# Dilated attention with tokens in class order from psum on; gamma products on VectorE

## The chip, the cores and the metric

The kernel runs on one core of one Trainium2 chip. The time is the device time of that core in microseconds (us); lower is better. Engines are named as in the profile: PE (TensorE), DVE (VectorE), ACT (ScalarE), POOL (GpSimd), SP (SyncE, which issues most transfers).

## What is computed

One sequence of 512 tokens with 1024 features passes through two blocks in fp32. The first block has a layer with an RWKV-7 and a MoBA mixer, a squared-ReLU MLP, a layer of dilated attention and another MLP. The second block has four mixers side by side (S5, HGRN2, FoX, mLSTM), an output projection and a SwiGLU layer. Two places matter here.

Dilated attention has 8 heads of 128 features, and for each head three queries, one for each pair of span and dilation, (128, 1), (512, 4) and (2048, 16), with one key and one value:

```python
q, k = _partial_rotary(q, pos), _partial_rotary(kv[0], pos)
for g, (span, dilation) in enumerate(DIL_PAIRS):
    o, l = _dilated_window_branch(q[:, g], k, v, span, dilation)
wts = jax.nn.softmax(jnp.stack(lses, axis=0), axis=0)
o = jnp.einsum('gbht,gbhtd->bhtd', wts, jnp.stack(outs, axis=0))
```

With dilation 4 a token sees tokens of its own class, its position mod 4; with dilation 16, of its own class mod 16. The rotary part turns the first 32 of the 128 features.

In the second block each branch ends in a norm with gain: `h = h + rms_norm(mix, ln_mix_post)` after the output projection, and `h = h + rms_norm(ff, ln_ffn_post)` at the end, where `rms_norm` is x times the reciprocal root of the mean square, times gamma.

## The kernel before

All large projections are done as three fp32r matmuls for each 128 x 512 product (high part by high, high by low, low by high; lines 272 to 274, 249 to 251, 356 to 358). Weights come by DMA on SP's queue into `wr`, ACT rounds them to the high part `wh` (L228), and DVE or POOL subtracts for the low part `wl` (L230).

In `dilated` (L1215) the projections of the eight heads are a stream of tasks on PE, five for a head, in the order key, three queries, value (j = 3, 0, 1, 2, 4). Each task's result in psum is copied out by ACT into `dz` (`evac`, L1228). For queries and the key the rotary part follows on the first 32 partitions: DVE shuffles halves into `dsh` (L1238), POOL multiplies `dsh` by the sines (L1243), DVE multiplies `dz` by the cosines (L1244), POOL adds the two (L1245). Before, only the query of dilation 1 (j = 0) is stored by class: within each tile of 128 tokens first the 32 tokens of class 0, then of class 1 and so on, so its copy (L1233) and its products have operands with steps of four fp32. The others lie in the order of the tokens.

`head` (L1250) then does one head. It transposes the value (`dipv`, L1257). For each tile t of 128 queries `score` makes a row of scores in psum, `disc`: one matmul with the near keys (L1265), and for the two dilated queries four small matmuls each, one for a class r, which write 32 psum partitions and 32 (t + 1) columns (L1268). Both operands of these are read with a step of four fp32:

```python
lhsT=q[:, t * P + r : t * P + P : 4], rhs=k[:, r : 4 * n : 4], start=True, stop=True,
tile_position=(0, 32 * r),
```

DVE adds the mask and takes the maximum (L1284), ACT does the exponential (L1290), and DVE makes the weights `e` over all keys of the tiles up to t (`de`): reciprocal (L1292), class masks scaled (L1294), the sum of the two dilated parts (L1295), its spread to four classes (L1297), and the near part (L1301). PE transposes `e` (`dipt`, L1305), DVE and ACT copy the halves (`dpt`, L1310 and L1311), and PE multiplies with the value (`dipo`, L1314). ACT writes the head's output back in token order with a step of four (L1316). The order on PE is set by a small planner (`race`, L305) that puts the steps of a head between matmuls of the projection stream; the numbers that a head yields are its estimates. Each engine executes in a fixed order of its own.

`post_part` (L1005) handles one half (c = 0 or 1, 512 features) of one tile of 128 tokens of a branch: ACT squares it and sums the squares (`square`, L990); for c = 0 ACT copies it from psum (L1012, if the destination is another tile) and POOL multiplies by gamma in place (L1013), for c = 1 DVE multiplies (L1017). `post_norm` (L1020) takes the reciprocal root on DVE (`rsqrt1`, lines 166 to 174) and adds both halves into the residual stream (L1029). It serves the output projection of the second block, whose four tiles of the half c = 0 are finished in psum early (`K.po`), and the SwiGLU layer, whose sums `facc` lie in SBUF. The transposes for the next projection are `ptr` (L980).

Of the kernel before, what the change touches and what calls it, by code (L numbers as in the profile page):

```python
# [15 lines left out]
ALU = mybir.AluOpType  # L16
# [27 lines left out]
def make_consts():  # L44
# [28 lines left out]
    q_ = (4 * ii + cc)[:, None]  # L73
    neg = lambda ok: np.where(ok, 0.0, NEG)
    add("dil", "cls", cc[:, None] == np.arange(4))
    for t in range(NT):
        n = 32 * (t + 1)
        j = np.arange(n)[None, :]
        i_ = (32 * t + ii)[:, None]
        own = neg(c_ <= q_)  # L80
        near = own if t == 0 else np.concatenate([neg(c_ >= q_), own], 1)
        add("dil", f"dil{t}", np.concatenate([near, neg(j <= i_), neg((j <= i_) & ((i_ - j) % 4 == 0))], 1))
# [828 lines left out]
class Stream:  # L911
# [93 lines left out]
    def post_part(self, pool, t, c, src, g, dst):  # L1005
# [4 lines left out]
        if c == 0:  # L1010
            if dst is not src:
                self.K.nc.scalar.copy(dst, src)  # L1012
            self.K.nc.gpsimd.tensor_tensor(dst, dst, g[:, 0:512], op=ALU.mult)  # L1013
        else:
            if dst is src:
                dst = pool.tile([P, 512], F32, name="sg")
            self.K.nc.vector.tensor_tensor(dst, src, g[:, 512:D], op=ALU.mult)  # L1017
# [197 lines left out]
def dilated(K, ctx, S, x, win, rope_d, yT, ys, w_out):  # L1215
# [12 lines left out]
    def evac(h, j):  # L1228
        def f(ps):
            z = s2.tile([P, T], F32, name=f"dz{j}")  # L1230
            if j == 0:
                z4 = z.rearrange("p (t r i) -> p t r i", t=NT, r=4)
                nc.scalar.copy(z4, ps.rearrange("p (t i r) -> p t r i", t=NT, r=4))  # L1233
            else:
                nc.scalar.copy(z, ps)
            if j < 4:
                sh = s2.tile([32, T], F32, name="dsh")
                nc.vector.stream_shuffle(sh, z[0:32], swap)  # L1238
                zr, sr, c_, s_ = z[0:32], sh, rope[:, 0, :], rope[:, 1, :]
                if j == 0:  # L1240
                    zr, sr = z4[0:32], sh.rearrange("p (t r i) -> p t r i", t=NT, r=4)
                    c_, s_ = (a.rearrange("p (t i r) -> p t r i", t=NT, r=4) for a in (c_, s_))
                nc.gpsimd.tensor_tensor(sr, sr, s_, op=ALU.mult)  # L1243
                nc.vector.tensor_tensor(zr, zr, c_, op=ALU.mult)  # L1244
# [5 lines left out]
    def head(h, L):  # L1250
        while any((h, j) not in R for j in range(5)):
            yield None
        k, q0, q1, q2, vt = (R[h, j] for j in (3, 0, 1, 2, 4))
        v = s2.tile([P, NT, P], F32, name="dv")
# [6 lines left out]
        def score(t):  # L1261
# [4 lines left out]
            for g, q in ((0, q1), (1, q2)):  # L1266
                for r in range(4):
                    nc.tensor.matmul(  # L1268
                        ps[32 * r : 32 * r + 32, n0 + g * n : n0 + g * n + n],
                        lhsT=q[:, t * P + r : t * P + P : 4], rhs=k[:, r : 4 * n : 4], start=True, stop=True,  # L1270
# [1113 lines left out]
```

## Time and profile before

| | |
|---|---|
| median of the runs | 2234.99 us (3 runs, 2234.35 to 2239.33) |
| the profiled execution, its own time | 2230.15 us |
| its span, first to last instruction | 2228.0 us |
| PE busy | 2160.5 us (97%) |
| DVE busy | 1265.1 us (57%) |
| ACT busy | 758.6 us (34%) |
| POOL busy | 382.0 us (17%) |
| mean granted clock of PE | 0.987 of 2.4 GHz |
| chain that ended last | PE 79%, DVE 10%, issue 4%, ACT 3%, DMA 2%, POOL 2% |

Busy time is the time in which an engine executes instructions of the program. The chain that ended last is followed back from the last instruction, at each step to what released it. A row of a timeline has the start in us from the span's start, the length in us, the engine, the line, the operation, the tiles out<-in, shapes and the number of records; in brackets, how long the engine had been idle and what released it. A PE row of x16 is sixteen records in a row, and an fp32 matmul has two records. The granted clock is what the chip allows PE: 1.00 is 2.4 GHz, 0.50 is 1.2 GHz. A row of busy time by stretch has the stretch's start and end and its length, then the busy us (and records) of PE, of PEld (PE's weight loads), DVE, ACT and POOL, then the mean granted clock, the busy share of the DMA engines and the GB/s that they moved. A row of the groups by line has, behind the shapes and the count, the busy us and the mean ns of one, and then the us of idle time before them; in the groups of a stage, the waits are a total, their number and the longest, in us.

### The profile page before, as it was taken

What the parts mean: (1) busy time and instruction counts of PE and PEld (TensorE: products, weight loads), DVE (VectorE), ACT (ScalarE), POOL (GpSimd) and SP (SyncE); (2) the same over time, 40 slices, a digit from 0 to 9 for tenths busy, and PEclk for the clock granted to TensorE, in tenths of its full rate; (3) what the DMA queues carried; (4) which work ended last, traced back from release to release, by engine and by line L of the source; (5) the groups of instructions that cost most, each with busy time, mean ns of one, the idle gap of its engine ahead of it and who ended that gap; (6) DMA issues with size and microseconds to landing.
All of it is one profiled execution on the core that took longest, in us unless ns stands there. A gap on an engine that the chain in (4) does not pass through costs nothing.

```text
span 2228.0 us, 37413 instructions
## 1 busy us (share of the span) xinstructions
PE 2160.5 (97%) x15646; PEld 1709.3 (77%) x15646; DVE 1265.1 (57%) x2528; ACT 758.6 (34%) x1218; POOL 382.0 (17%) x399
## 2 busy tenths in 40 slices
PE   8999999999999999999999999998999998999997
PEld 6666667888878877777788888877667778888886
DVE  6576666764444765656574444466755566344445
ACT  4332333423322433333342233235434354222221
POOL 0011111370056242332130000011320021000001
PEclk9999999999999999999999999998899999999999
DMA  4111114342333322222243233213211232233321
GB/s 142 49 40 40 49 40 170 97 131 95 100 100 113 126 77 67 67 68 66 86 139 94 90 104 95 93 45 132 63 45 46 92 104 95 95 97 98 99 76 38
DMA packets 56088, 192.80 MB, mean 87 GB/s; under 512 B 8208, under 2 KB 8720, under 8 KB 55408
## 3 DMA queue, kind: packets, MB, share of 16 engines
q1 hardware_dynamic: 52384, 184.11, 25.6%
q0 software_dynamic: 3536, 6.32, 0.9%
q8 instruction: 122, 2.00, 0.4%
q14 instruction: 46, 0.38, 0.1%
HBM read 181.98 MB, written 8.39 MB: 85 GB/s over the span
## 4 chain that ended last, share of the span: by engine, by line
PE 79%; DVE 10%; issue 4%; ACT 3%; DMA 2%; POOL 2%; SPq 0%; DVEq 0%; ACTq 0%; POOLq 0%
PE gemm L272 6%; PE mlpo L356 6%; PE mlpo L357 6%; PE mlpo L358 6%; PE gemm L273 5%; PE gemm L274 5%; PE mlps L249 4%; PE mlps L250 4%; PE mlps L251 4%; PE ffg L250 2%; PE ffg L251 2%; PE ffg L249 2%; PE ffu L250 2%; PE ffu L251 2%; PE ffu L249 2%
## 5 line engine op out<-in xcount | busy, mean ns | idle before, releaser
L228 ACT CAST wh<-wr 128x1024 fp32r<-128x1024 f32 (+1 forms) x311 | 323.4, 1044 | 762.3 <-PE mlpo L358 247.5
L230 DVE TENSOR_TENSOR wl<-wr,wh 128x1024 fp32r<-128x1024 f32 (+1 forms) x285 | 354.9, 1246 | 359.9 <-ACT wh L228 270.2
L272 PE MATMUL gemm<-acth,wh 128*128 128x512 f32 (+1 forms) x672 | 306.1, 456 | 7.8 <-ACT acth L238 6.4
L274 PE MATMUL gemm<-acth,wl 128*128 128x512 f32 (+1 forms) x672 | 271.8, 404 | 4.5 <-DVE wl L230 4.5
L273 PE MATMUL gemm<-actl,wh 128*128 128x512 f32 (+1 forms) x672 | 272.4, 405 | 0.0
L356 PE MATMUL mlpo<-wh,mlph 128*128 128x512 f32 x688 | 270.2, 393 | 0.3 <-DVE xres L1039 0.3
L357 PE MATMUL mlpo<-wl,mlph 128*128 128x512 f32 x688 | 269.6, 392 | 0.0
L358 PE MATMUL mlpo<-wh,mlpl 128*128 128x512 f32 x688 | 269.4, 392 | 0.0
L249 PE MATMUL mlps<-acth,wh 128*128 128x512 f32 x448 | 176.3, 394 | 0.0
L251 PE MATMUL mlps<-acth,wl 128*128 128x512 f32 x448 | 176.2, 393 | 0.0
L250 PE MATMUL mlps<-actl,wh 128*128 128x512 f32 x448 | 176.1, 393 | 0.0
L272 PEld LDWEIGHTS gemm<-acth,wh 128*128 128x128 f32 (+1 forms) x672 | 128.9, 192 | 59.1 <-issue 24.7
L274 PEld LDWEIGHTS gemm<-acth,wl 128*128 128x128 f32 (+1 forms) x672 | 128.9, 192 | 36.0 <-DVE wl L230 5.8
L356 PEld LDWEIGHTS mlpo<-wh,mlph 128*128 128x128 f32 x688 | 129.4, 188 | 29.3 <-DVE xres L1039 0.4
L358 PEld LDWEIGHTS mlpo<-wh,mlpl 128*128 128x128 f32 x688 | 129.1, 188 | 29.1 <-DVE mlpl L239 0.2
L357 PEld LDWEIGHTS mlpo<-wl,mlph 128*128 128x128 f32 x688 | 129.2, 188 | 28.6
L230 POOL TENSOR_TENSOR wl<-wr,wh 128x1024 fp32r<-128x1024 f32 (+1 forms) x26 | 71.2, 2763 | 446.0 <-ACT wh L228 424.1
L273 PEld LDWEIGHTS gemm<-actl,wh 128*128 128x128 f32 (+1 forms) x672 | 129.9, 193 | 22.9 <-issue 4.4
L1039 DVE SCALAR_TENSOR_TENSOR xres<-xres,mlpo 128x512 f32<-128x512 f32 x120 | 82.1, 685 | 105.3 <-PE mlpo L358 104.3
L251 PEld LDWEIGHTS mlps<-acth,wl 128*128 128x128 f32 x448 | 84.1, 188 | 19.7
L250 PEld LDWEIGHTS mlps<-actl,wh 128*128 128x128 f32 x448 | 84.2, 188 | 19.4
L249 PEld LDWEIGHTS mlps<-acth,wh 128*128 128x128 f32 x448 | 84.1, 188 | 19.5
(617 smaller groups left out, 3901.9 us busy)
## 6 DMA issues: line engine op xcount, KB each, us to landing
wr<-mlp_w SPq DMA_DIRECT2D x128, 512.0 KB, 3.6
wr<-ffn_w SPq DMA_DIRECT2D x66, 512.0 KB, 3.5
wr<-c_w_in SPq DMA_DIRECT2D x40, 512.0 KB, 3.6
wr<-ab_w_in SPq DMA_DIRECT2D x25, 512.0 KB, 3.6
wr<-w_in SPq DMA_DIRECT2D x24, 512.0 KB, 3.7
wr<-ab_w_out SPq DMA_DIRECT2D x8, 512.0 KB, 3.9
wr<-c_w_out SPq DMA_DIRECT2D x8, 512.0 KB, 3.7
wr<-w_out SPq DMA_DIRECT2D x8, 512.0 KB, 3.9
```

The costliest lines, as they stand in the source:

```text
L228: nc.scalar.copy(hi, raw)
L230: eng.tensor_tensor(lo, raw, hi.bitcast(F32), op=ALU.subtract)
L249: nc.tensor.matmul(ps, lhsT=hs, rhs=a, start=start and k == 0, stop=False)
L250: nc.tensor.matmul(ps, lhsT=hs, rhs=b, start=False, stop=False)
L251: nc.tensor.matmul(ps, lhsT=ls, rhs=a, start=False, stop=stop and k == n - 1)
L272: nc.tensor.matmul(ps[0:m], lhsT=h[:, 0:m], rhs=xh[:, k, :], start=k == 0, stop=False)
L273: nc.tensor.matmul(ps[0:m], lhsT=h[:, 0:m], rhs=xl[:, k, :], start=False, stop=False)
L274: nc.tensor.matmul(ps[0:m], lhsT=l[:, 0:m], rhs=xh[:, k, :], start=False, stop=k == n - 1)
L356: nc.tensor.matmul(ps, lhsT=a, rhs=h[:, c0 : c0 + n], start=start and k == 0, stop=False)
L357: nc.tensor.matmul(ps, lhsT=a, rhs=l[:, c0 : c0 + n], start=False, stop=False)
L358: nc.tensor.matmul(ps, lhsT=b, rhs=h[:, c0 : c0 + n], start=False, stop=stop and k == kt - 1)
L1039: self.K.nc.vector.scalar_tensor_tensor(xs, xs, f, ps, op0=ALU.mult, op1=ALU.add, accum_out=self.sums[:, t, c : c + 1])
```

## The change

Dilated attention: every projection is copied out of psum in class order, the key, the queries of the dilations 4 and 16 and the value like the query of dilation 1. The table of cosines and sines is reordered on the host in the same way (`rope_c`), so that the rotary products have plain operands. The small score matmuls read 32 neighbouring query tokens and, of the keys, runs of 32 neighbouring tokens, one from each tile. The mask of the near part and the spread of the weights (`e`) follow that order of keys. The number of instructions, their order and their shapes in dilated attention stay as they are.

`post_part`: for both halves DVE multiplies by gamma straight from the source, psum or SBUF. The copy on ACT and the product on POOL are gone.

```diff
+    k_ = (4 * (np.arange(P) % 32) + np.arange(P) // 32)[None, :]
...
-        own = neg(c_ <= q_)
-        near = own if t == 0 else np.concatenate([neg(c_ >= q_), own], 1)
+        own = neg(k_ <= q_)
+        near = own if t == 0 else np.concatenate([neg(k_ >= q_), own], 1)
...
-        if c == 0:
-            if dst is not src:
-                self.K.nc.scalar.copy(dst, src)
-            self.K.nc.gpsimd.tensor_tensor(dst, dst, g[:, 0:512], op=ALU.mult)
-        else:
-            if dst is src:
-                dst = pool.tile([P, 512], F32, name="sg")
-            self.K.nc.vector.tensor_tensor(dst, src, g[:, 512:D], op=ALU.mult)
+        if c and dst is src:
+            dst = pool.tile([P, 512], F32, name="sg")
+        self.K.nc.vector.tensor_tensor(dst, src, g[:, 512 * c : 512 * c + 512], op=ALU.mult)
...
-            if j == 0:
-                z4 = z.rearrange("p (t r i) -> p t r i", t=NT, r=4)
-                nc.scalar.copy(z4, ps.rearrange("p (t i r) -> p t r i", t=NT, r=4))
-            else:
-                nc.scalar.copy(z, ps)
+            nc.scalar.copy(z.rearrange("p (t r i) -> p t r i", t=NT, r=4), ps.rearrange("p (t i r) -> p t r i", t=NT, r=4))
...
-                zr, sr, c_, s_ = z[0:32], sh, rope[:, 0, :], rope[:, 1, :]
-                if j == 0:
-                    zr, sr = z4[0:32], sh.rearrange("p (t r i) -> p t r i", t=NT, r=4)
-                    c_, s_ = (a.rearrange("p (t i r) -> p t r i", t=NT, r=4) for a in (c_, s_))
-                nc.gpsimd.tensor_tensor(sr, sr, s_, op=ALU.mult)
-                nc.vector.tensor_tensor(zr, zr, c_, op=ALU.mult)
+                nc.gpsimd.tensor_tensor(sh, sh, rope[:, 1, :], op=ALU.mult)
+                nc.vector.tensor_tensor(z[0:32], z[0:32], rope[:, 0, :], op=ALU.mult)
...
+        k4 = k.rearrange("p (t r i) -> p t r i", t=NT, r=4)
...
-                        ps[32 * r : 32 * r + 32, n0 + g * n : n0 + g * n + n],
-                        lhsT=q[:, t * P + r : t * P + P : 4], rhs=k[:, r : 4 * n : 4], start=True, stop=True,
+                        ps[32 * r : 32 * r + 32, n0 + g * n : n0 + g * n + n].rearrange("p (b i) -> p b i", i=32),
+                        lhsT=q[:, t * P + 32 * r : t * P + 32 * r + 32], rhs=k4[:, 0 : t + 1, r], start=True, stop=True,
...
-                e.rearrange("p (j r) -> p j r", r=4), bc(s_[:, n0 : n0 + n], 4), cl.unsqueeze(1).to_broadcast([P, n, 4]), op=ALU.mult
+                e.rearrange("p (b r i) -> p b r i", r=4, i=32),
+                s_[:, n0 : n0 + n].rearrange("p (b i) -> p b i", i=32).unsqueeze(2).to_broadcast([P, t + 1, 4, 32]),
+                cl.unsqueeze(1).unsqueeze(3).to_broadcast([P, t + 1, 4, 32]), op=ALU.mult,
...
-                    wk = dilated(K, c3, S, a2, A["c_w_in"], A["rope"], y, ys, A["c_w_out"])
+                    wk = dilated(K, c3, S, a2, A["c_w_in"], A["rope_c"], y, ys, A["c_w_out"])
...
+    arr["rope_c"] = np.ascontiguousarray(ROPET.reshape(32, 2, NT, 32, 4).transpose(0, 1, 2, 4, 3).reshape(32, 2 * T))
```

On ACT at block 2's output projection (`pjps` is a projection in psum, `mix` the destination, `sqj` the squares, `wh` a weight's high part) the order was this before:

```order
L990 ACTIVATE sqj,pn_16742<-pjps 128x512
L1012 COPY mix<-pjps 128x512
L990 ACTIVATE sqj,pn_16747<-pjps 128x512
L1012 COPY mix<-pjps 128x512
L990 ACTIVATE sqj,pn_16752<-pjps 128x512
L1012 COPY mix<-pjps 128x512
L990 ACTIVATE sqj,pn_16757<-pjps 128x512
L1012 COPY mix<-pjps 128x512
L228 CAST wh<-wr 128x1024 x4
L990 ACTIVATE sqj,pn_16742<-pjps 128x512
```

and is now this:

```order
L991 ACTIVATE sqj,pn_16742<-pjps 128x512
L991 ACTIVATE sqj,pn_16746<-pjps 128x512
L991 ACTIVATE sqj,pn_16750<-pjps 128x512
L229 CAST wh<-wr 128x1024
L991 ACTIVATE sqj,pn_16754<-pjps 128x512
L229 CAST wh<-wr 128x1024 x2
L991 ACTIVATE sqj,pn_16742<-pjps 128x512
L229 CAST wh<-wr 128x1024
```

The four copies are gone, and one of the four weight casts stands behind the first square of the half c = 1 (the second `pn_16742`).

On DVE at the same place (`wl` is a weight's low part, `ymix` the mixers' output, `gaing` gamma), before:

```order
L1688 SCALAR_TENSOR_TENSOR ymix<-mgt,mgb 128x512
L230 TENSOR_TENSOR wl<-wr,wh 128x1024
L239 TENSOR_TENSOR actl<-ymix,acth 128x512
L230 TENSOR_TENSOR wl<-wr,wh 128x1024 x3
L1017 TENSOR_TENSOR mix<-pjps,gaing 128x512
L166 TENSOR_SCALAR rs_16790<-pn_16742 128x1
```

and now:

```order
L1680 SCALAR_TENSOR_TENSOR ymix<-mgt,mgb 128x512
L231 TENSOR_TENSOR wl<-wr,wh 128x1024
L240 TENSOR_TENSOR actl<-ymix,acth 128x512
L231 TENSOR_TENSOR wl<-wr,wh 128x1024 x2
L1013 TENSOR_TENSOR mix<-pjps,gaing 128x512 x2
L231 TENSOR_TENSOR wl<-wr,wh 128x1024
L1013 TENSOR_TENSOR mix<-pjps,gaing 128x512 x3
L167 TENSOR_SCALAR rs_16786<-pn_16742 128x1
```

Four products are added, two of them ahead of the last weight split.

On DVE at the end of the kernel, between the first and the second tile of tokens (`rs` is the reciprocal root, `sg` the product of the half c = 1, `xres` the residual stream), before:

```order
L1156 TENSOR_TENSOR facc<-facc,mlpo 128x512
L173 TENSOR_SCALAR rs_19419<-rs_19419 128x1
L174 TENSOR_SCALAR rs_19419<-rs_19419 128x1
L1029 SCALAR_TENSOR_TENSOR xres<-facc,rs_19419,xres 128x512
L1029 SCALAR_TENSOR_TENSOR xres<-sg,rs_19419,xres 128x512
L1156 TENSOR_TENSOR facc<-facc,mlpo 128x512
L1017 TENSOR_TENSOR sg<-facc,gaing 128x512
```

and now:

```order
L1152 TENSOR_TENSOR facc<-facc,mlpo 128x512
L174 TENSOR_SCALAR rs_19415<-rs_19415 128x1
L175 TENSOR_SCALAR rs_19415<-rs_19415 128x1
L1025 SCALAR_TENSOR_TENSOR xres<-facc,rs_19415,xres 128x512
L1013 TENSOR_TENSOR facc<-facc,gaing 128x512
L1025 SCALAR_TENSOR_TENSOR xres<-sg,rs_19415,xres 128x512
L1152 TENSOR_TENSOR facc<-facc,mlpo 128x512
L1013 TENSOR_TENSOR sg<-facc,gaing 128x512
```

The product of the next tile's half c = 0 stands between the two sums of this tile.

## Rows read from the trace of the kernel before

**Rows 1.** Busy time by stretch: dilated attention; block 2's second projection and norm.
```profile
770.00:1110.00 340.00, 327.02 (x2004) 259.28 (x2002) 206.63 (x445) 121.08 (x214) 101.15 (x65) 0.98 0.23 72
...
1812.00:1848.00 36.00, 28.14 (x130) 22.16 (x129) 25.82 (x63) 19.66 (x43) 24.00 (x11) 1.00 0.45 148
```

**Rows 2.** PE's waits, 770 to 1110 us: total, times, longest.
```profile
PE dipo L1314 <- DVE dpt L1310: 6.5, 4, 1.7
...
PE disc L1268 <- POOL dz L1245: 3.1, 1, 3.1
```

**Rows 3.** PE's timeline, the score groups of one head: start us, us, instruction.
```profile
923.73 0.47 PE L1268 MATMUL disc<-dz,dz 128*32 128x32 f32 x16
...
925.23 0.68 PE L1268 MATMUL disc<-dz,dz 128*32 128x64 f32 x16
...
930.99 0.91 PE L1268 MATMUL disc<-dz,dz 128*32 128x96 f32 x16
...
938.04 1.13 PE L1268 MATMUL disc<-dz,dz 128*32 128x128 f32 x16
```

**Rows 4.** PE's s5k and s5y; record lengths in ns (min/median/max; last row the mean).
```profile
658.17 0.49 PE L2165 MATMUL s5k<-s5CAt,s5W 128*32 128x32 f32 x32
...
1577.36 0.43 PE L1954 MATMUL s5y<-sF,sCA 128*32 128x63 f32 x16
...
L1954 PE MATMUL s5y<-sF,sCA x256: 218/218/315, 1575.4 to 1617.5; 128*32 128x63 f32 x128
...
L1268 PE MATMUL disc<-dz,dz 128*32 128x64 f32 x128 | 5.5, 302 | 0.0
```

**Rows 5.** Groups by line, DVE, 770 to 1125: busy us, mean ns, idle.
```profile
L1297 DVE TENSOR_TENSOR de<-ds,dcl 128x512 f32<-128x512 f32 x8 | 5.5, 693 | 0.3
```

**Rows 6.** Timelines of DVE and PE, head 1 of eight, t = 2.
```profile
856.41 0.53 DVE L1295 TENSOR_TENSOR ds<-ds 128x96 f32<-128x96 f32 x1
...
857.60 0.28 DVE L1310 COPY dpt<-dipt 128x128 f32<-128x128 f32 x1
...
857.93 0.79 PE L1314 MATMUL dipo<-dpt,dv 128*128 128x128 f32 x4
```

**Rows 7.** Timelines of DVE and POOL, the same head, t = 3.
```profile
862.37 1.08 DVE L1244 TENSOR_TENSOR dz<-dz,rope 32x512 f32<-32x512 f32 x1
...
863.45 1.56 DVE L1295 TENSOR_TENSOR ds<-ds 128x128 f32<-128x128 f32 x1
...
862.41 2.45 POOL L1243 TENSOR_TENSOR dsh<-dsh,rope 32x512 f32<-32x512 f32 x1 [5.58 <-DVE dstat L1287]
...
864.94 1.26 POOL L1245 TENSOR_TENSOR dz<-dz,dsh 32x512 f32<-32x512 f32 x1
```

**Rows 8.** Busy time by stretch, after the wait in that head.
```profile
868.20:871.40 3.20, 3.20 (x10) 2.52 (x10) 0.00 (x0) 0.73 (x1) 0.00 (x0) 0.50 0.02 5
```

**Rows 9.** Groups by line, ACT, 770 to 1110 us.
```profile
L1235 ACT COPY dz<-gemm 128x512 f32<-128x512 f32 x29 | 16.8, 579 | 0.0
...
L1233 ACT COPY dz<-gemm 128x512 f32<-128x512 f32 x7 | 4.1, 583 | 0.0
```

**Rows 10.** Timelines of ACT, POOL and PE around block 2's second projection.
```profile
1820.84 2.00 ACT L228 CAST wh<-wr 128x1024 fp32r<-128x1024 f32 x2 [1.74 <-DMA wr<-ffn_w]
...
1813.84 6.04 POOL L1013 TENSOR_TENSOR mix<-mix,gaing 128x512 f32<-128x512 f32 x4 [98.45 <-ACT mix L1012]
...
1838.16 8.45 POOL L230 TENSOR_TENSOR wl<-wr,wh 128x1024 fp32r<-128x1024 f32 x3 [0.23 <-ACT wh L228]
...
1833.21 1.06 PE L980 MATMUL ptr<-consts,prea 128*128 128x128 f32 x8 [1.67 <-DVE rs L174]
```

**Rows 11.** DVE's timeline in the tail.
```profile
2211.61 1.78 DVE L1029 SCALAR_TENSOR_TENSOR xres<-sg,rs,xres 128x512 f32<-128x512 f32 x1
...
2214.02 0.69 DVE L1017 TENSOR_TENSOR sg<-facc,gaing 128x512 f32<-128x512 f32 x1
...
2224.33 0.74 DVE L1029 SCALAR_TENSOR_TENSOR xres<-sg,rs,xres 128x512 f32<-128x512 f32 x1
```

## The prediction

> **What bounds the kernel now.** I read the busy times of the stages first, then PE's waits, then the timeline of the places that the diff touches. In the stretch of dilated attention PE is busy for 327.0 of 340 us, DVE for 207 and POOL for 101: the stage belongs to PE [rows 1]. PE's whole list of waits there is short: 6.5 us in four waits of `dipo` for the copies `dpt`, and 3.1 us at the start for POOL's `dz` [rows 2]. So what takes less of PE's time comes off the end, as long as the engines that feed PE come along. The stage after the second block's mixing is another matter: of 36 us PE is busy for 28.1 [rows 1], and the chain through DVE and ACT sets the pace. At the very end PE has finished and DVE alone runs the last products and sums.
>
> **The score matmuls.** The change leaves PE's instructions and their order alone; it changes where 256 score matmuls (eight heads, four tiles t, two groups, four classes r) read. Before, stationary and moving operand take every fourth fp32; after, both are contiguous (the moving one in runs of 32). The profile shows each of these fp32 matmuls as two records, so a group of eight is 16 records. In one head the four groups, of 32, 64, 96 and 128 columns, last 0.47, 0.68, 0.91 and 1.13 us [rows 3]; the other heads read the same within 0.03.
>
> What would they last unstrided? Block 2 and its preparation have two column-tiled fp32 groups of the same shape (128 rows by 32 columns, strips side by side) with contiguous operands: `s5y`, 16 records of 63 columns in 0.43 us, and `s5k`, 32 records of 32 columns in 0.49 us [rows 4]. Less one record's own length (0.22 us, and about 0.20 for the shorter one) the records of `s5y` follow each other every 14 ns and those of `s5k` every 9.5 ns, against (0.68 - 0.30)/15 = 25 ns for the strided 64 columns. For 16 records I take 0.49 - 16 x 0.0095 = 0.34 us at 32 columns, 0.43 at 64, and 0.12 more for every further 32 columns (15 steps growing by 7 ns, and a little for the last record): 0.55 and 0.67. The savings are 0.13 + 0.25 + 0.36 + 0.46 = 1.20 us per head, **9.6 us in eight heads**. Bounds: 8 if the last record grows as in the strided groups, 10.5 if the step from `s5k` to `s5y` (0.09 for 31 columns) holds further up; and nothing if the stride is not what costs (a rival).
>
> The Trainium skill speaks against it: "TensorE: Matmul & The Clock Gate", section "Wait — 56ns, not 53.3ns?", says that matmuls start no closer than about 25 ns however few columns they have. By that the groups of 32 and 64 columns would gain nothing, the larger ones would stop near 25 ns, and the sum would be an estimated 4 us. The 9.5 ns of `s5k` do not agree with it, for strips side by side.
>
> **What gives part of it back.** At t = 2 the softmax chain does not start at the score: DVE first shuffles the next projection, which hangs on a copy that precedes the score in PE's order, and the copy L1310 of t = 1 is queued behind t = 2's products. It ends at 857.88, and PE takes it at 857.93 [rows 6]. PE will be there 0.36 us sooner, DVE will not, so a wait of 0.3 us appears. Seven heads have 0.05 to 0.2 us of slack at this place, the last has enough. Seven times 0.27: **1.9 us back**.
>
> At t = 3, in four heads (the four waits of [rows 2]), DVE is late already. There the j = 0 rope product L1244 takes 1.08 us, being strided, against 0.69 for a contiguous product of 512 [rows 7, 11]. POOL's product waits behind it for the port, then takes 1.4 us (1.26 for the contiguous sum after it), and holds up L1295 (1.56 us) in turn [rows 7]. With everything contiguous DVE gains 0.4, POOL 0.15, and the score's being there sooner 0.2; so DVE comes 0.75 sooner and PE 0.46: the wait of 1.6 us falls to 1.3. **Four times 0.3, and about 0.5 at the first head**, where POOL's serial chain ends in the wait of 3.1 us: 1.7 us.
>
> After three of these four waits, and after the one of 3.1 us, the granted clock is 0.50 for a stretch of at least 3.2 us, that is 1.2 GHz in place of 2.4 [rows 8], the one near 868; the others begin near 807, 984 and 1025. Each costs half its length, 1.6 us. The waits get shorter but do not vanish; I let **one stretch go: 1.6 us**, ends 0 and 6.4.
>
> Terms at nothing. All 40 copies out of psum, in place of 8, now read in steps of four: 583 ns against 579 [rows 9]. "PSUM — Partial Sum Buffer" in the Trainium skill, section "Specifications (TRN2)", says that any non-contiguous pattern slows matmuls significantly; the rows show 4 ns for these reads, and `s5y`, which writes psum in steps of eight (L1955), is the quick group. If the copies took the strided product's factor, 1.08/0.69, they would each cost 0.33 us, on PE's path at two places per head: 5 us. The product `e` (L1297, 693 ns [rows 5]) gets a four-level pattern that no row shows. It runs at the pace of a contiguous product already, so it cannot gain; with L1244's factor it loses 0.3 to 0.4 us at t = 2 and in half of the heads at t = 3, 4 us in all. I take 0 for both: no row shows a loss without strided elements on the SBUF side.
>
> **The products with gamma, block 2's mixing.** Four ACT copies (L1012) and four POOL products go, four DVE products of 0.69 us [rows 11] come. They lie at 1813 to 1817, where DVE has idle time; the weight split `wl` among them is later by at most 0.6 us, but no longer fights POOL's products. On ACT, the first square of the second half stood behind four weight casts, of which two were held for a DMA until 1820.84 and then took 2.00 us [rows 10]; after, one of the four is placed behind it. It comes 0.85 us sooner, or 2 us if the transfer comes sooner too: POOL's weight splits, which free the buffers, start when its 6.04 us of products are gone [rows 10], so 2 us sooner. That chain ends in `ptr`, for which PE waits 1.67 us [rows 10]. I take **1.4 us**; bounds 3 (the next wait shortened too) and -2, since POOL's later splits, 2.8 us each [rows 10], may fall on other DVE products than now.
>
> **The tail.** POOL's four products go to DVE, 0.69 us each, in place of holding up the sum L1029, which takes 1.78 us under POOL's product and 0.74 alone [rows 11]. The first lies in idle time. Three times 1.04 - 0.69: **1.1 us**, bounds 0.5 and 1.6.
>
> **Sum** against the profiled execution, whose 2230.15 us lie 2.15 over its span of 2228.0: -9.6 + 1.9 - 1.7 - 1.6 - 1.4 - 1.1 = -13.5, so 2216.6. The median of the runs shown, 2234.99, is 4.84 above that execution; with the same difference the forecast is **2221.5 us**.
>
> **Rivals.**
> - *The stride costs PE nothing.* The groups grow by 0.22 us per 32 columns [rows 3], 0.43 ns per record and column, near one fp32 per cycle at 2.4 GHz: the strips could share one reader, and contiguous operands would change nothing. Against it stands `s5y`, at 14/63 = 0.22 ns. Then 1.7 + 1.4 + 1.1 us remain: about 2231. Chance 0.09.
> - *Records cannot follow closer than now at 64 columns, 25 ns.* Groups of 32 and 64 stay, those of 96 and 128 fall from 37 and 48 ns to 25 and 28: 15 x 0.032 = 0.5 us per head, 4 us in place of 9.6, and 1 us less comes back: about 2226. Against it stands `s5k` [rows 4]. The Trainium skill has this rule in "TensorE: Matmul & The Clock Gate". Chance 0.05.
> - *POOL's splits collide worse in the mixing.* One more split of 2.8 us in front of a sum, and the 1.4 not won and a stretch at 1.2 GHz behind it: 5.8 us lost, about 2227. Chance 0.05.
> - *Slower: DVE is what PE waits for in every head.* At t = 2 POOL's addition delays L1295 in part, to 0.53 us [rows 6]; if the shifted times put it wholly in front, as at t = 3 (1.56), each of seven waits of 0.3 becomes 1.3, and the three heads without a wait at t = 3 get the 1.6 too: 7 x 1.0 + 3 x 1.6 = 12 us. It decides against the change once stretches at 1.2 GHz follow, as after waits of 1.6: three to ten of them, 5 to 16 us, and the one that I let go is not won. Net +5 to +16, about 2245. For it: three heads already read like this at t = 3. Against it: POOL's work gets shorter, not longer. Chance 0.05.
>
> **The numbers.** The forecast has 0.76. Its own range is 2213 (all four slow stretches gone, the mixing at 3) to 2228 (8 us from the scores, 4 of waits, a mixing that loses). 0.2% is 4.5 us, about what a measurement of this kernel can tell from no change, so faster means under 2230.5: the forecast, the second and third rival, but for 0.02, make 0.84. Same: the first rival and that rest, 0.11. Slower 0.05. A range of 2213 to 2231 leaves out the slower rival, half of the first and about 0.06 below.
>
> **What would show it.** Right: score groups of about 0.34, 0.43, 0.55 and 0.67 us; short new waits of `dipo` for L1310 at t = 2; L1029 at 0.75 us throughout the tail; `ptr` waiting less. Wrong: groups still of 0.68 and 1.13 us; waits of `dipo` above 10 us in sum; five or more stretches at 0.50 in dilated attention; a sum L1029 above 3 us in the mixing.

## The result, and the profile after

The changed kernel takes 2210.85 us, the median of 4 runs (2210.03 to 2214.23), against 2235.07 for the kernel before (4 runs, 2234.35 to 2239.33). The ratio is 0.9897, with a 95% interval of 0.9884 to 0.9910. It is faster, as forecast, but by 24.2 us where 13.5 were forecast, and 2.15 us below the range.

The profiled executions differ by less: 2230.15 against 2210.03, 20.1 us. As PE issues the same matmuls in the same order in both, each matmul's start can be set against that of its twin, which gives the lead of the changed kernel at every point: none up to 800 us; 17.0 us gained in dilated attention; 3.1 lost between its end and 1300 us; 3.3 gained in block 2's first stage; 0.8 in the mixing and 2.2 in the tail. The third and fourth of these lie where nothing was edited, and are the clock: two stretches at 1.2 GHz that begin at 1093.3 and 1124.1 us and that the first profile of before does not have, and 23.9 us at that clock in block 2's first stage where it was 30.7.

The page of the changed kernel, its busy times (span 2207.9 us):

```profile
PE 2146.2 (97%) x15646; PEld 1701.9 (77%) x15646; DVE 1259.3 (57%) x2536; ACT 756.1 (34%) x1214; POOL 363.3 (16%) x391
```

PE, DVE, ACT and POOL all have less to do; PE's 14 us are most of the gain.

**Dilated attention.** The busy time of the stage, and the list of PE's waits in it, of the changed kernel (columns as in [rows 1] and [rows 2]):

```profile
770.00:1093.00 323.00, 312.02 (x2003) 249.84 (x2003) 199.40 (x445) 121.11 (x214) 97.00 (x65) 1.00 0.24 76
```

```profile
PE dipo L1306 <- DVE dpt L1302: 5.3, 8, 1.1
PE disc L1258 <- POOL dz L1234: 2.5, 1, 2.5
PE pjps L357 <- ACT acth L239: 1.8, 1, 1.8
PE dipv L1247 <- ACT dz L1228: 1.1, 2, 0.6
```

PE has 15 us less to do, its clock is 1.00 in place of 0.98, and there are eight waits for DVE in place of four, though shorter in sum [rows 1, 2]. The stretch shown ends just before one at half the clock, 1.5 us behind PE's wait of 1.8 us for ACT (`acth`), which had none behind it before:

```profile
1093.40:1096.60 3.20, 3.20 (x9) 2.52 (x8) 2.83 (x7) 0.00 (x0) 0.00 (x0) 0.50 0.77 294
```

The timeline of PE, the score groups of one head:

```profile
1027.87 0.33 PE L1258 MATMUL disc<-dz,dz 128*32 128x32 f32 x16
1029.23 0.43 PE L1258 MATMUL disc<-dz,dz 128*32 128x64 f32 x16
1034.72 0.54 PE L1258 MATMUL disc<-dz,dz 128*32 128x96 f32 x16
1041.95 0.65 PE L1258 MATMUL disc<-dz,dz 128*32 128x128 f32 x16
```

These stand against 0.47, 0.68, 0.91 and 1.13 us [rows 3]. From the start of each group to the start of what follows, the 32 groups take 16.05 us after and 26.81 before; 0.57 of the difference is the first head's wait for `dz`, so the scores themselves give 10.2 us.

The waits at the second head, t = 1 and t = 2 of its `dipo`, and ACT's copy between:

```profile
854.21 0.79 PE L1306 MATMUL dipo<-dpt,dv 128*128 128x128 f32 x4 [0.28 <-DVE dpt L1302]
862.46 1.17 PE L1306 MATMUL dipo<-dpt,dv 128*128 128x128 f32 x6 [1.05 <-DVE dpt L1302]
```

```profile
862.49 0.37 ACT L1303 COPY dpt<-dipt 128x256 f32<-128x256 f32 x1 [3.33 <-DVE dpt L1302]
```

These are the places that the forecast calls t = 2 and t = 3, after the score in front of them. The wait of 0.28 is the new one of the forecast. The list has it in four heads (0.24 to 0.28), but it came in all seven: from the start of the matmul in front to the start of this `dipo` PE takes 0.23 to 0.39 us longer than before in each of them, 2.2 in sum. The list counts PE idle only from the modelled end of the matmul in front. The wait of 1.05 was 1.59, one of the four of [rows 2]. Before, the granted clock was 0.50 behind it [rows 8]; now the same place reads 1.00:

```profile
863.60:866.80 3.20, 3.20 (x16) 2.58 (x15) 0.90 (x1) 1.53 (x2) 0.00 (x0) 1.00 0.02 5
```

None of the four stretches at 1.2 GHz in dilated attention is left. From start to start against their twins, the matmuls give these parts of the 17.0 us: 10.2 are the scores, 0.6 the first head's wait (3.1 to 2.5), and 6.0 the matmuls that ran at 1.2 GHz in the four stretches before. What `dipo` gains at its longer wait in four heads (2.2 in front, 0.5 inside the groups) it loses again at the new one in seven (2.2 and 0.4).

The copies out of psum and the product `e` cost nothing, as forecast (ACT and DVE, groups by line, 785 to 1095 us; [rows 5, 9]):

```profile
L1228 ACT COPY dz<-gemm 128x512 f32<-128x512 f32 x36 | 20.8, 578 | 0.0
```

```profile
L1287 DVE TENSOR_TENSOR de<-ds,dcl 128x512 f32<-128x512 f32 x8 | 5.5, 692 | 0.3
```

**The mixing.** ACT's square of the second half, POOL's splits, DVE's sum and PE's transposes, each from the timeline of its engine:

```profile
1803.16 0.59 ACT L991 ACTIVATE sqj<-pjps 128x512 f32<-128x512 f32 x1
...
1803.33 4.77 POOL L231 TENSOR_TENSOR wl<-wr,wh 128x1024 fp32r<-128x1024 f32 x2 [1.91 <-ACT wh L229]
...
1806.64 2.67 DVE L1025 SCALAR_TENSOR_TENSOR xres<-mix,rs,xres 128x512 f32<-128x512 f32 x2
...
1814.36 1.07 PE L981 MATMUL ptr<-consts,prea 128*128 128x128 f32 x8 [0.39 <-DVE rs L175]
```

The first squares of the first half start 17.2 us before their twins, this one 19.6 us (1822.74 before): it comes 2.4 us sooner. Two casts that wait for a DMA stand before it in both kernels; the first one's transfer is there 2.8 us sooner in the same sense (1800.88 against 1820.84 [rows 10]). POOL's splits, which now lie under more of the two sums L1025, stretch them to 2.67 us (1.87 before), which takes 0.8 of it back. PE's wait for `ptr` falls from 1.67 us [rows 10] to 0.39.

**The tail**, DVE's timeline of one tile of tokens (small rows of the reciprocal root left out by the dots):

```profile
2194.92 0.69 DVE L1013 TENSOR_TENSOR sg<-facc,gaing 128x512 f32<-128x512 f32 x1
...
2197.80 0.68 DVE L1013 TENSOR_TENSOR facc<-facc,gaing 128x512 f32<-128x512 f32 x1
...
2198.65 0.75 DVE L1025 SCALAR_TENSOR_TENSOR xres<-facc,rs,xres 128x512 f32<-128x512 f32 x1
2199.32 0.68 DVE L1152 TENSOR_TENSOR facc<-facc,mlpo 128x512 f32<-128x512 f32 x1
2199.91 0.75 DVE L1025 SCALAR_TENSOR_TENSOR xres<-sg,rs,xres 128x512 f32<-128x512 f32 x1
2200.69 0.69 DVE L1013 TENSOR_TENSOR sg<-facc,gaing 128x512 f32<-128x512 f32 x1
```

All sums take 0.75 us; the one under POOL's product took 1.78 [rows 11]. Before, the product that follows the one of 2214.02 [rows 11] came at:

```profile
2220.60 0.69 DVE L1017 TENSOR_TENSOR sg<-facc,gaing 128x512 f32<-128x512 f32 x1
```

### The profile page after: what moved, and what is told of

Same layout as the page of the kernel before. It is cut to its first block, busy times and chain, and to the rows that moved or that the text cites. A ratio compares the mean times of both kernels' runs of the same rounds, so it can differ in the third digit from the quotient of the medians.

```text
span 2207.9 us, 37394 instructions
## 1 busy us (share of the span) xinstructions
PE 2146.2 (97%) x15646; PEld 1701.9 (77%) x15646; DVE 1259.3 (57%) x2536; ACT 756.1 (34%) x1214; POOL 363.3 (16%) x391
## 4 chain that ended last, share of the span: by engine, by line
PE 79%; DVE 11%; issue 4%; ACT 3%; DMA 2%; POOL 1%; SPq 0%; DVEq 0%; ACTq 0%; POOLq 0%
PE gemm L273 6%; PE mlpo L357 6%; PE mlpo L358 6%; PE mlpo L359 6%; PE gemm L274 5%; PE gemm L275 5%; PE mlps L250 5%; PE mlps L251 5%; PE mlps L252 5%; PE ffg L251 2%; PE ffg L252 2%; PE ffg L250 2%; PE ffu L251 2%; PE ffu L252 2%; PE ffu L250 2%
```

## The experiments

**The two parts alone.** First the part in dilated attention, with `post_part` as before:

```diff
-        if c and dst is src:
-            dst = pool.tile([P, 512], F32, name="sg")
-        self.K.nc.vector.tensor_tensor(dst, src, g[:, 512 * c : 512 * c + 512], op=ALU.mult)
+        if c == 0:
+            if dst is not src:
+                self.K.nc.scalar.copy(dst, src)
+            self.K.nc.gpsimd.tensor_tensor(dst, dst, g[:, 0:512], op=ALU.mult)
...
```

> Only the part in dilated attention; the products with gamma stay as before (POOL multiplies the half c = 0, ACT copies it). Theory: dilated attention holds 17 of the 20 us by which the two profiled executions differ (10.2 of it in the score groups, start to start), so about 2217 us in the median, ratio 0.992; the tail still has sums of 1.78 us under POOL's product. Rival: the gamma products hold more than the tail's 2.2 and the mixing's 0.9 us, since the medians differ by 24 us and not by 20: then 2220 or more.

Measured: 2218.23 us (6 runs), ratio 0.9937 (0.9921 to 0.9952), 14.6 us below the kernel before of the same session (2232.83, 19 runs). Its profile gains 17.4 us between the start of the first head and the last `dipo`, no stretch at half the clock in between, and nothing in the tail:

```profile
2210.00 1.75 DVE L1030 SCALAR_TENSOR_TENSOR xres<-sg,rs,xres 128x512 f32<-128x512 f32 x1
```

Then the other way round, the kernel before with the products of `post_part` changed:

> Only the products with gamma; dilated attention as before, with strided scores. Theory: 2.2 us in the tail (about 0.8 for each of three tiles of tokens) and about 1 in the mixing, so about 2232 us, ratio 0.9986; dilated attention keeps its four stretches at half the clock and its four waits of 1.6 us. Rival: the four us that the medians differ more than the profiles belong to this part: about 2228. Rival 2: the four stretches in dilated attention come and go by themselves: fewer than three of them here.

Measured: 2230.06 us (11 runs), ratio 0.9987 (0.9977 to 0.9997), 2.8 us less. In its profile the tail gives 2.2 us, and the transposes of the mixing come 1.75 us sooner, of which a later stretch at half the clock takes a part. Dilated attention has its waits of 1.6 us and three stretches, not the same ones: one stands behind a wait that had none in the first profile, and the first head's wait has none. So both parts stand where the traces put them. Their sum is 17.4 us, below the 24 of the first measurement; the last experiment takes that up.

**Which operand's step costs.** The stationary one in steps of four again, then the moving one:

```diff
-                        lhsT=q[:, t * P + 32 * r : t * P + 32 * r + 32], rhs=k4[:, 0 : t + 1, r], start=True, stop=True,
+                        lhsT=q[:, t * P + r : t * P + P : 4], rhs=k4[:, 0 : t + 1, r], start=True, stop=True,
```

> The changed kernel, with the stationary operand of the 256 score matmuls read in steps of four again, the moving one contiguous. The layout is left as it is, so queries meet other tokens' keys: the scores of the dilated parts are changed. Theory M (the moving operand's step is what costs): the groups of 16 records keep 0.33, 0.43, 0.54 and 0.64 us. Rival S (the weight loads cost, 138 ns in steps of four against about 108): the groups come back to 0.47 to 1.13, or at least 0.03 us x 16 records longer in the small ones, 0.8 at 32 columns. Rival B (each operand has a part): all four groups between.

```diff
-                        lhsT=q[:, t * P + 32 * r : t * P + 32 * r + 32], rhs=k4[:, 0 : t + 1, r], start=True, stop=True,
+                        lhsT=q[:, t * P + 32 * r : t * P + 32 * r + 32], rhs=k[:, r : 4 * n : 4], start=True, stop=True,
```

> The changed kernel, with the moving operand of the score matmuls read in steps of four again, the stationary one contiguous. Again queries meet other tokens' keys, the scores of the dilated parts are changed. Theory M: the groups are back at 0.47, 0.68, 0.91 and 1.13 us, 10 us in eight heads, and the profile has a span of about 2218 us. Rival S: they keep 0.33 to 0.64. Rival B: between, and the two together make the 10 us.

PE's timeline of one head with the stationary operand strided:

```profile
955.36 0.45 PE L1258 MATMUL disc<-dz,dz 128*32 128x32 f32 x16
956.83 0.48 PE L1258 MATMUL disc<-dz,dz 128*32 128x64 f32 x16
962.39 0.57 PE L1258 MATMUL disc<-dz,dz 128*32 128x96 f32 x16
969.45 0.68 PE L1258 MATMUL disc<-dz,dz 128*32 128x128 f32 x16
```

and with the moving one:

```profile
954.37 0.42 PE L1258 MATMUL disc<-dz,dz 128*32 128x32 f32 x16
955.82 0.65 PE L1258 MATMUL disc<-dz,dz 128*32 128x64 f32 x16
961.55 0.87 PE L1258 MATMUL disc<-dz,dz 128*32 128x96 f32 x16
968.58 1.10 PE L1258 MATMUL disc<-dz,dz 128*32 128x128 f32 x16
```

From start to start the 32 groups take 17.77 and 24.84 us, against 16.05: 1.7 us for the stationary operand, 8.8 for the moving one, 10.5 together. The moving operand's step costs per column: the growth for 32 columns is 0.22 us with it, and 0.11 without. The stationary one costs in the small group, 0.12 us of 16 weight loads that take 145 ns each in place of 109 (PE's weight loads, 800 to 1100 us, with the stationary operand strided, and in the changed kernel):

```profile
L1258 PEld LDWEIGHTS disc<-dz,dz 128*32 128x32 f32 x512 | 12.0, 145 | 11.5 <-issue 7.9 <-POOL dz L1234 2.6
```

```profile
L1258 PEld LDWEIGHTS disc<-dz,dz 128*32 128x32 f32 x512 | 9.6, 109 | 11.6 <-issue 8.0 <-POOL dz L1234 2.6
```

So rival B is right: each operand has a part, and together they make the 10 us; the moving one has five sixths of it. The single times of these two runs, 2219.59 and 2220.49 us, lie only 0.9 us apart where the groups lie 7 apart: the second has shorter waits of `dipo` (3.8 us in sum in place of 5.0), and the first more stretches at half the clock elsewhere (two at 287 and 400 us, where no edit is). In dilated attention itself the second loses 4.9 us to the changed kernel and not 8.8: PE comes later to `dipo` and loses 2.6 us less in front of it and 1.1 us less inside its groups. A score matmul that is slower hides part of DVE's lateness.

**The waits for DVE.** The kernel before, then the changed one, with ACT alone copying `dpt`:

```diff
-            if h0:
-                nc.vector.tensor_copy(pT[:, 0:h0], pt[:, 0:h0])
-            nc.scalar.copy(pT[:, h0 : 4 * n], pt[:, h0 : 4 * n])
+            nc.scalar.copy(pT[:, 0 : 4 * n], pt[:, 0 : 4 * n])
```

> The kernel before, with strided scores, but the transposed weights dpt are copied by ACT alone, so PE no longer waits for DVE's queue at dipo. Theory (a wait of 1.6 us is what the stretch at half the clock follows): the four waits go, 6.5 us, and with them three of the four stretches, some 1.2 to 1.5 us each, the one behind POOL's dz at the first head stays: about 2225 us. Rival (the stretches fall where they fall): 6.5 us alone, about 2228.5, with three or four stretches left. Second rival: ACT, queued behind the exponentials, is late in turn and PE waits for ACT instead: no gain, 2235 or more.

> The changed kernel with the same edit: ACT alone copies dpt. Theory: the eight waits of dipo for DVE, 5.3 us in sum, go, and there is no stretch at half the clock behind them to win: about 2205.5 us, ratio to before 0.9868. Rival: ACT is late in turn, at 1 us or more in each head: about 2211 or more. Second rival: stretches at half the clock follow from the position in time and not from waits: two to four in dilated attention again, 2208 to 2212.

Measured: 2222.95 us (8 runs), ratio 0.9957 (0.9942 to 0.9971), and 2205.93 us (4 runs), ratio 0.9883 (0.9866 to 0.9900). Both medians are near the theory's 2225 and 2205.5, by parts that it did not have. From start to start against their twins, the matmuls of the first gain 13.3 us in dilated attention: 5.2 in front of `dipo`, 3.3 inside its groups and 4.6 from the clock (one stretch is left, behind the first head's wait). Its profile loses 4.5 of them again to stretches where nothing was edited, at 398, 1098 and 1129 us. PE's waits in the second:

```profile
PE disc L1258 <- POOL dz L1234: 2.5, 1, 2.5
PE pjps L357 <- ACT acth L239: 1.8, 1, 1.8
PE dipo L1306 <- ACT dpt L1303: 1.0, 3, 0.4
PE dipv L1247 <- ACT dz L1228: 0.9, 2, 0.5
```

The `dipo` of the second head, ACT's copy first, then PE:

```profile
857.56 0.48 ACT L1303 COPY dpt<-dipt 128x384 f32<-128x384 f32 x1 [0.95 <-PE dipt L1297]
```

```profile
858.70 0.83 PE L1306 MATMUL dipo<-dpt,dv 128*128 128x128 f32 x6
```

One copy of 384 columns on ACT is done before PE comes, and the group takes 0.83 us where it took 1.17. Most of that difference is a stop inside the group, which the list of waits does not show: in the changed kernel PE starts on DVE's half and stops again for ACT's, which began when DVE's had ended (862.49, above). From start to start the groups of `dipo` take 20.8 us in the changed kernel and 17.6 with ACT alone: 3.1 us, which lay beside the 5.3 us of the list and which the theory did not count. At one granted clock this kernel takes 9 us less than the changed one: 2206.8 us at 0.987 (3 runs), where the changed one takes 2215.8 (2 runs).

Does ACT's half wait because both halves are written into one tile? The changed kernel with two:

```diff
+            pT, pA = s2.tile([P, 2 * P], F32, name="dpt"), s2.tile([P, 2 * P], F32, name="dpa")
...
-            nc.scalar.copy(pT[:, h0 : 4 * n], pt[:, h0 : 4 * n])
+            nc.scalar.copy(pA[:, 0 : 4 * n - h0], pt[:, h0 : 4 * n])
```

> The changed kernel, but DVE's half and ACT's half of dpt lie in two tiles (dpt and dpa). In the changed kernel ACT's half starts only when DVE's has ended (862.49 us behind DVE's copy of 862.12 that takes 0.28), and PE stops a second time inside the groups of dipo: 0.54 us from the first matmul to the next work where four take 0.36, 0.86 to 0.93 where six take 0.59, 3.1 us over all heads. Theory (one half waits for the other because both write one tile): with two tiles ACT's half is done first, the groups fall to 0.36 and 0.59, the waits for DVE's half stay at 1.05 and 0.25: 3.1 us less, about 2208 us. Rival (ACT is late by itself): the groups stay at 0.54 and 0.9, 2211.

Measured: 2218.12 us (5 runs), ratio 0.9921 (0.9895 to 0.9947), and the groups unchanged at 0.54 and 0.93. The theory fell: ACT still starts behind DVE's copy (which ends at 864.87), into another tile. ACT's timeline:

```profile
864.96 0.37 ACT L1303 COPY dpa<-dipt 128x256 f32<-128x256 f32 x1 [3.33 <-DVE dpt L1302]
```

The program itself has ACT wait for DVE's semaphore there. What the halves still share is the source, the tile `dipt` in psum; two psum tiles were not tried, so that cause is argued and not shown. The median is 5 to 7 us above the other two of the changed kernel; the work on every engine is the same, and the profile has a longer stretch at half the clock behind the first head's wait, and more of them in block 2.

Last, the first head's wait for POOL, with the version that has ACT's copies:

```diff
-                nc.gpsimd.tensor_tensor(z[0:32], z[0:32], sh, op=ALU.add)
+                (nc.gpsimd if h else nc.vector).tensor_tensor(z[0:32], z[0:32], sh, op=ALU.add)
```

> The changed kernel with dpt copied by ACT alone, and the rotary sums of the first head's four tiles on DVE in place of POOL. Theory: POOL's chain of eight operations, which ends in PE's wait of 2.5 us for dz, is half as long, and that wait goes: about 2203.5 us, 2.4 less than with ACT's copies alone. Rival: DVE's weight splits, queued behind the four sums, are late by as much: 2206 or more.

Measured: 2200.53 us (6 runs), ratio 0.9862 (0.9836 to 0.9888): the fastest kernel of this study, ahead of both. The wait is halved and not gone: DVE's last sum has to wait for POOL's product by the sines, which takes 3.28 us (from 799.28) while DVE runs a product and a weight split. PE's wait, and DVE's row:

```profile
PE disc L1258 <- DVE dz L1234: 1.2, 1, 1.2
```

```profile
802.59 0.68 DVE L1234 TENSOR_TENSOR dz<-dz,dsh 32x512 f32<-32x512 f32 x1 [1.16 <-POOL dsh L1232]
```

Of the 5.4 us between the two medians the trace shows 1.3 here and 1.5 from a stretch at 1083.5 us in the former profile that the latter does not have. The rest is not accounted for by any edit: three of the four runs of the former have a granted clock of 0.987, five of the six of the latter 0.989 or more.

**The waits and the clock.** That waits of 1.6 us bring the stretches at 1.2 GHz, and that shorter ones don't, was argued so far from one pair of profiles. So the waits were made long again, with contiguous scores, by a second table for the rotary products of j = 0 (`q4` and `tk` give steps of four for j = 0 alone):

```diff
-                nc.vector.tensor_tensor(z[0:32], z[0:32], rope[:, 0, :], op=ALU.mult)
+                nc.vector.tensor_tensor(q4(z[0:32]), q4(z[0:32]), tk(0), op=ALU.mult)
...
+tk = lambda w: ropt[:, w, :].rearrange("p (t i r) -> p t r i", t=NT, r=4) if j == 0 else rope[:, w, :]
```

> The changed kernel, but the rotary products of the query j = 0 (L1232, L1233) take the sines and cosines from a table in token order, in steps of four, as before; the results are the same numbers, and one transfer more loads the second table. The score matmuls stay contiguous, the order on each engine stays. Theory: the strided product delays DVE by 0.4 us and POOL's with it, so the four longer waits of dipo grow from 1.05 to between 1.6 and 2.0 us, and stretches at half the clock follow three or four of them again: about 2217 us. Rival (the stretches had no cause in the waits): the waits grow and no stretch comes: about 2213. Second rival: the step in the products costs DVE nothing: waits of 1.05, 2211.

Measured: 2222.41 us (4 runs), ratio 0.9946 (0.9927 to 0.9965). DVE's and PE's timeline at the second head, and the stretch behind the wait:

```profile
862.69 1.07 DVE L1233 TENSOR_TENSOR dz<-dz,ropt 32x512 f32<-32x512 f32 x1
863.77 1.55 DVE L1285 TENSOR_TENSOR ds<-ds 128x128 f32<-128x128 f32 x1
...
867.17 0.28 DVE L1302 COPY dpt<-dipt 128x128 f32<-128x128 f32 x1
```

```profile
867.51 1.17 PE L1306 MATMUL dipo<-dpt,dv 128*128 128x128 f32 x6 [1.67 <-DVE dpt L1302]
```

```profile
868.50:871.70 3.20, 3.20 (x16) 2.61 (x15) 0.73 (x1) 1.53 (x2) 0.00 (x0) 1.00 0.02 5
```

The products are back at 1.07 us, DVE's sum L1285 under POOL's product at 1.55, the four waits at 1.7: the strided rotary products cost what [rows 7] showed. But behind none of the four waits the clock falls. Only the first head's wait, now 3.2 us, has a stretch. The theory that the wait alone decides fell in this run. The time fits none of the three either, 5 us above the theory's. Set against the changed kernel's profile, 7.3 of 16.5 us are lost in dilated attention, 5.1 of them at `dipo` and at the first head's wait; most of the others lie in block 2, where nothing was edited. A second profile of this kernel, and one of the kernel before, unchanged:

> The changed kernel with the rotary products of j = 0 strided again, for a second profile: contiguous scores and waits of 1.7 us. Theory C: no stretch at half the clock behind the four waits of dipo, as in the first profile of it (one may stand behind the first head's wait for dz, 3.2 us). Rival (chance): two or more.

> The kernel before, unchanged, for a second profile. Theory C (strided scores and waits of 1.6 us together bring the stretches): three or four stretches at half the clock behind the waits of dipo and dz in dilated attention, as in the first profile and in that with gamma's products alone; the stretches in the second block's first stage differ from the first profile by one or two. Rival (position in time): two or fewer in dilated attention.

In the second profile of the former (2222.94 us) one of the four waits of 1.7 us has a stretch behind it; in that of the latter (2230.22 us) one of the four of 1.6, and the first head's. Three or four were expected there: a miss, and by its number the rival's case. The same place as in [rows 8], in the second profile of the kernel before, after a wait of 1.61 us:

```profile
869.70:872.90 3.20, 3.20 (x16) 2.63 (x16) 0.70 (x1) 1.53 (x2) 0.00 (x0) 1.00 0.02 5
```

Over all profiles of the study, counted as a stretch at 0.50 that begins in a wait or up to 4 us after its end (`pjps` is PE's wait for ACT at the end of the stage, which no edit touches):

| PE's waits in dilated attention | waits | with a stretch behind |
|---|---|---|
| `dipo`, 0.9 to 1.1 us (changed kernel and its variants, 6 profiles) | 24 | 0 |
| `dipo`, 1.6 to 1.7 us, contiguous scores (2 profiles) | 8 | 1 |
| `dipo`, 1.6 to 1.7 us, strided scores (3 profiles) | 12 | 7 |
| `pjps`, 1.8 us (14 profiles) | 14 | 8 |
| `dz`, 2.5 us (7 profiles) | 7 | 2 |
| `dz`, 3.1 to 3.2 us (6 profiles) | 6 | 5 |

Waits of 1.6 us and more often have a stretch behind them, though the share does not grow evenly with their length; none came behind the 24 short ones, and which of the waits between get one changes from run to run of the same kernel. That strided scores add to it (7 of 12 against 1 of 8) is suggested by these few, not settled: behind the wait of 1.8 us kernels with contiguous scores have one in 5 of 10 profiles, those with strided scores in 3 of 4.

**The changed kernel again**, in more runs:

> The changed kernel, unchanged, in more runs. Theory A (the parts add up, and part of the first difference of 24 us was a draw of the clock): dilated attention alone gave 14.6 us and gamma's products 2.8, so 17.4 less than before, about 2215.5 us beside a before of 2233; the profile has none or one stretch at half the clock in dilated attention. Theory B (the first measurement stands): 2211 us, 22 to 24 us less than before. A stretch behind the waits of 1.05 us in none of four heads by either; behind the first head's wait of 2.5 us in at most one.

Measured: 2213.11 us (6 runs, 2205.46 to 2217.29), ratio 0.9915 (0.9898 to 0.9933), 19.6 us less than the kernel before of that session. It lies between the two theories. With the first four, ten runs of the changed kernel have a median of 2212.0; the kernel before has 2232.8 in 54 runs, from 2225.46 to 2242.09. So the difference is some 20 to 21 us, and the 24.2 of the first comparison were partly a draw. What is drawn shows in the granted clock that each run lists. Runs at one clock (of the 50 and 10 that list it):

| mean granted clock of a run | before, mean (runs) | changed, mean (runs) | difference |
|---|---|---|---|
| 0.987 | 2231.8 (10) | 2215.8 (2) | 16.0 |
| 0.988 | 2230.1 (7) | 2215.1 (1) | 15.0 |
| 0.989 | 2227.8 (2) | 2211.9 (5) | 15.9 |

At an equal clock the change is worth 15 to 16 us. The other 5 go with the clock, which lies lower before (between 0.984 and 0.988 in most runs) than after (0.987 to 0.992). All ten runs of the changed kernel list 0.987 or more and 19 of the 50 of the kernel before, so part of the higher clock is the change's own; how much of the 5 us is not shown.

## Why the prediction was wrong

The direction and the mechanism held; the size did not. Of the 10.65 us between 2221.5 and 2210.85, 6.6 lie between the profiles (13.5 forecast, 20.1 measured) and 4.0 in the step from profile to median. The term that failed is the one for the stretches at half the clock, 1.6 us where dilated attention gave 6.0; the next are the longer waits at `dipo`, the tail and the step to the median.

- *The scores, 9.6 us, bounds 8 to 10.5.* Right: 10.2, with groups of 0.33, 0.43, 0.54 and 0.65 us against 0.34, 0.43, 0.55 and 0.67. Taking the spacing of the records from `s5y` and `s5k` [rows 4] gave each of them within 0.02 us. The rival by which the step costs nothing is out, and so is the one of 25 ns: at 32 columns 16 records of some 0.20 us fit into 0.33 us, one every 9 ns. The Trainium skill's rule behind that rival ("TensorE: Matmul & The Clock Gate", section "Wait — 56ns, not 53.3ns?") does not agree with strips side by side.
- *New waits at t = 2, 1.9 us back.* Right: 2.2 us in seven heads in front of `dipo`, 0.23 to 0.39 each, and 0.4 inside its groups. The list of waits shows half of it.
- *Shorter waits at t = 3 and at the first head, 1.7 us.* Too small: the four fell from 1.6 to 1.05 and not to 1.3, and the first head's by 0.6: 2.8 us, and 0.5 more inside the groups of `dipo` in the heads that do not wait in front of it. PE comes there 0.5 us sooner as reckoned, so DVE comes about 1.0 sooner and not 0.75. The working gave POOL 0.15 us; its product of j = 0 takes 1.78 us in place of 2.45 [rows 7], and DVE's sum L1285 behind it 0.96 in place of 1.56. With strided rotary products alone the sum is back at 1.55.
- *"I let one stretch go: 1.6 us", ends 0 and 6.4.* This is the step that failed most. All four went, and the clock gave 6.0 us in that stage, 1.5 for each. The text took a shortened wait for one that keeps its stretch; behind waits of 0.9 to 1.1 us not one of 24 had any. And it read four stretches from one profile as the kernel's own, where the next profile of the same kernel has two. The stretches after dilated attention and in block 2, +3.1 and -3.3 us between the profiles, cancelled by chance.
- *Copies and `e` at nothing.* Right: 578 and 692 ns. `s5y`, which writes psum in steps of eight, takes the 0.43 us [rows 4] that the score group of 64 columns takes now, which writes neighbouring columns.
- *The mixing, 1.4 us, bounds 3 and -2.* The way was right, 0.8 us are left of it: PE's transposes come 1.7 us sooner, and a longer stretch at half the clock behind them takes 0.9. In seven of the ten profiles with the new products PE spends two or three times as long at half the clock there as in the four without them, a price that the sum did not have. The rival of worse collisions is there in small, 0.8 us at the sums L1025, and paid for by the earlier square.
- *The tail, 1.1 us, bounds 0.5 and 1.6.* Too small: 2.2, the same in the profile with gamma's products alone. The step was "three times 1.04 - 0.69". DVE's time from one tile to the next falls by 0.51, 0.63 and 0.81 us (the last: 5.77 from 2194.92 to 2200.69, against 6.58 from 2214.02 to 2220.60), not by 0.35, so 0.2 to 0.5 us of the product's 0.69 are paid. In the third tile it stands among the short operations of the reciprocal root, each of which takes the result of the one before, and makes their chain 0.47 us longer. The last tile, which has no product, takes 0.27 less: in the third and the last, where `facc` is added before the second sum (L1152, 2199.32), the next chain starts 0.2 us sooner behind the product `sg`.
- *Profile to median.* "With the same difference the forecast is 2221.5 us": the profiled execution of before lay 4.84 us under its median and that of the change 0.82. The first is at the fast end of 54 runs whose times follow their granted clock; a part of that distance was not the kernel's to carry over.
- *Slower, DVE in every head:* no sign of it. DVE's contiguous products shortened POOL's hold, as the argument against it said.

## What to carry to other kernels

Where many small matmuls read an operand in steps, lay the tokens out at the copy that leaves psum: here that copy and its readers on other engines cost nothing more, and the moving operand's step alone was 8.8 of 10.5 us. A wait of PE costs its length and, from 1.6 us on, often the clock behind it; but read such stretches over several profiles before a sum counts on them, and compare medians at an equal granted clock. A product placed in a chain of short operations costs less than its length, and a copy split over two engines gains nothing where the second one waits for the first.

## What was not expected

- The stationary operand's step costs as well: weight loads of 145 ns against 109, 0.12 us in a group of 16 with 32 columns, but 0.03 in one of 128 columns.
- The two halves of a copy out of one psum tile ran one after the other, on ACT and DVE, and PE stopped twice for them: 3.1 us in eight heads that no list of waits showed. Why the program orders them so is not shown.
- A wait of 1.6 us before the same matmul of the same program had a stretch at 1.2 GHz behind it in one execution [rows 8] and none in the next.
- The time of one program on one core spreads over 17 us in 54 runs (2225.46 to 2242.09), together with its granted clock: 2235.3 us on average at 0.984 (11 runs), 2230.1 at 0.988 (7 runs).
